# Computing the first tile of a gated elementwise kernel in four pieces of half a row in place of two rows

## Chip, cores, metric

One NeuronCore of one Trainium2 chip. The metric is the device time of one execution in microseconds (us). "Span" is the time from the first to the last instruction in a profile; the measured time is about 1.8 to 2.7 us more. The kernel before takes 935.15 us (median).

## The reference

```python
# x: 8192 x 8192, float32
def reference(x):
    a, b = np.split(x, 2, axis=-1)
    return a * (1 / (1 + np.exp(-b)))
```

268 MB are read and 134 MB are written; for each output there is one sigmoid and one multiply.

## The kernel before

The rows are cut into 32 tiles of 256 rows, two rows to a partition. A tile is one load of 8.39 MB (64 KB per partition, issued by SyncE), a sigmoid on ScalarE (ACT), a multiply on VectorE (DVE), and one store of 4.19 MB (32 KB per partition, issued by GpSimd, POOL). There are two input slots and two output slots, so loads 0 and 1 are issued at once, and load 2 waits for the last multiply of tile 0.

```python
    for i in range(n_tiles):
        ...                      # slots, views of rows and of the packed output
        load = nc.sync.dma_start(out=xs[i % SLOTS], in_=x_t[i])
        ...
        if i == 0:
            parts = [(slice(r, r + 1), slice(0, half)) for r in range(R)]      # two rows
        elif i < n_tiles - 1:
            parts = [(slice(0, R), slice(0, half))]                            # one piece
        else:
            w = half // 2                                                      # four pieces
            parts = [(slice(r, r + 1), slice(c * w, (c + 1) * w)) for r in range(R) for c in range(2)]
        for k, (r, c) in enumerate(parts):
            b = rows[:, r, 1, c]
            sig = nc.scalar.activation(out=b, in_=b, func=SIG)
            mul = nc.vector.tensor_mul(out=packed[:, r, c], in0=rows[:, r, 0, c], in1=b)
            ...                  # waits that follow from others are dropped
            if i == n_tiles - 1:
                ...              # the last tile stores each piece as it is done
        if i < n_tiles - 1:
            now["stores"].append(nc.gpsimd.dma_start(out=out_t[i], in_=os[i % SLOTS]))
```

Each odd tile's sigmoid, and each even tile's multiply, also waits for the store that had the same output slot two tiles ago.

## Time and profile before

| | kernel before |
|---|---|
| time, median of 6 (lowest to highest) | 935.15 us (935.06 to 935.74) |
| span of the profiled execution | 933.8 us |
| that execution's own time | 936.43 us |
| DVE, ACT busy | 30%, 24% |
| DMA engines busy | 9 tenths or more in 39 of 40 slices |

### The profile page before, as it was taken

The page shows a single profiled execution, that of the slowest core. Times are in us where ns is not written, and L with a number is a line of the kernel's source. Part 1 is how long each engine was busy: PE and PEld are TensorE (multiplying, and loading weights), DVE is VectorE, ACT ScalarE, POOL GpSimd, SP SyncE. Part 2 cuts the span into 40 slices and gives each one's busy share as a digit, 9 for nine tenths or more (in the row PEclk, how much of TensorE's full clock was granted, in tenths as well). Part 3 has the DMA queues.
Part 4 walks back from the last instruction along what each step waited for, and adds up shares of the span by engine and source line. Part 5 has one row for each costly group of instructions (what it writes and reads, how often), then busy time and mean ns, then how long its engine had stood idle before and what let it go on. Part 6 is the DMA issues. An engine that isn't in the chain of part 4 may idle for free.

```text
span 933.8 us, 259 instructions
## 1 busy us (share of the span) xinstructions
DVE 278.4 (30%) x36; ACT 226.6 (24%) x37; POOL 17.9 (2%) x37
## 2 busy tenths in 40 slices
DVE  0333213332133331333312333123331233311333
ACT  1223330233302333113331133311333203332023
POOL 0000000000000000000000000000000000000000
DMA  9999999999999999999999999999999999999998
GB/s 404 415 437 428 446 428 431 432 439 448 414 459 410 441 434 428 446 422 453 410 455 417 430 445 430 446 417 459 410 446 425 431 444 446 430 414 459 408 448 362
DMA packets 9649, 402.67 MB, mean 431 GB/s; under 512 B 1072, under 2 KB 1072, under 8 KB 1072
## 3 DMA queue, kind: packets, MB, share of 16 engines
q1 hardware_dynamic: 4896, 270.53, 67.1%
q0 software_dynamic: 4752, 132.12, 32.8%
q14 instruction: 1, 0.01, 0.0%
HBM read 268.44 MB, written 134.22 MB: 431 GB/s over the span
## 4 chain that ended last, share of the span: by engine, by line
DMA 73%; DVE 15%; ACT 12%; DVEq 0%; issue 0%; ACTq 0%
DMA x_sb<-in_x_dram 73%; DVE o_sb L68 15%; ACT x_sb L67 12%; DVEq L145 0%; ACTq L67 0%
## 5 line engine op out<-in xcount | busy, mean ns | idle before, releaser
L68 DVE TENSOR_TENSOR o_sb<-x_sb 128x8192 f32<-128x8192 f32 (+2 forms) x36 | 278.4, 7743 | 648.4 <-ACT x_sb L67 648.4
L67 ACT ACTIVATE x_sb<-x_sb 128x8192 f32<-128x8192 f32 (+2 forms) x36 | 225.3, 6269 | 696.0 <-DMA x_sb<-in_x_dram 696.0
L84 POOL DMA_DIRECT2D out_dram<-o_sb x31 | 16.7, 537 | 886.5 <-DVE o_sb L68 886.5
L67 ACT ACT_TABLE_LOAD x1 | 1.3, 1283 | 0.8 <-PEq L162 0.8
L81 POOL DMA_DIRECT2D out_dram<-o_sb x2 | 1.1, 533 | 18.6 <-DVE o_sb L68 18.6
L162 POOL MEMSET const-float32-0.0<- 128x1 f32 x1 | 0.1, 99 | 0.2 <-issue 0.2
L162 POOL MEMSET const-bfloat16-1.0<- 128x1 bf16 x1 | 0.1, 102 | 0.0
L162 POOL MEMSET const-float32-1.0<- 128x1 f32 x1 | 0.1, 99 | 0.0
L162 POOL MEMSET const-uint8-127<- 128x1 uint8 x1 | 0.1, 99 | 0.0
## 6 DMA issues: line engine op xcount, KB each, us to landing
out_dram<-o_sb POOLq DMA_DIRECT2D x31, 4096.0 KB, 36.1
out_dram<-o_sb POOLq DMA_DIRECT2D x2, 1024.0 KB, 5.3
out_dram<-o_sb SPq DMA_DIRECT2D x2, 1024.0 KB, 6.2
x_sb<-in_x_dram SPq DMA_DIRECT2D x32, 42.2
```

The costliest lines, as they stand in the source:

```text
L67: sig = nc.scalar.activation(out=b, in_=b, func=SIG)
L68: mul = nc.vector.tensor_mul(out=packed[:, r, c], in0=rows[:, r, 0, c], in1=b)
L81: store = queue.dma_start(out=out_t[i, :, cols], in_=os[i % SLOTS][:, cols])
L84: now["stores"].append(nc.gpsimd.dma_start(out=out_t[i], in_=os[i % SLOTS]))
L162: nc = _bacc.Bacc("TRN2", target_bir_lowering=False, num_devices=1)
```

## The change

The first tile takes the branch of the last tile: four sigmoids and four multiplies of half a row each in place of two and two of a row. A shorter first piece lets DVE start sooner, so tile 0 is finished sooner, and load 2 and store 0, which wait for it, are issued sooner.

```diff
-        if i == 0:
-            parts = [(slice(r, r + 1), slice(0, half)) for r in range(R)]
-        elif i < n_tiles - 1:
+        if 0 < i < n_tiles - 1:
             parts = [(slice(0, R), slice(0, half))]
         else:
             w = half // 2
```

## The prediction

> **What bounds the kernel now.** I read the page first, for the busy shares and the chain, then the chain in order of time, then the timeline of the start and of the end, and last the DMA of chosen stretches.
>
> The page says that no compute engine is near its limit, and that the DMA engines are full in all but the last of the 40 slices:
>
> ```profile
> DVE 278.4 (30%) x36; ACT 226.6 (24%) x37; POOL 17.9 (2%) x37
> ...
> DMA  9999999999999999999999999999999999999998
> ...
> DMA 73%; DVE 15%; ACT 12%; DVEq 0%; issue 0%; ACTq 0%
> ```
>
> The last line is a trap. The chain gives 27% of the span to DVE and ACT, which looks as if faster computing would shorten the end. The chain in order of time shows why it would not:
>
> ```profile
> 0.79 45.20 DMA x_sb<-in_x_dram
> ...
> 46.01 7.04 ACT x_sb L67
> ...
> 53.07 8.70 DVE o_sb L68
> ...
> 61.79 42.20 DMA x_sb<-in_x_dram
> ```
>
> The load issued at 61.79 takes 42.20 us to land, but the other slot's load is ahead of it in the same queue: that one lands at 75.0 (its sigmoid starts at 75.02), so this load only has the stretch from 75.0 to 104.0 for itself. A tile that is computed sooner would let its load wait longer in the queue, and it would land at the same time. The test is the DMA engines' share, stretch by stretch (columns: stretch, its length, busy time and count of DVE, ACT and POOL, clock, DMA share, GB/s):
>
> ```profile
> 0.00:34.60 34.60, 8.76 (x2) 8.40 (x3) 0.20 (x4) 1.00 1.00 424
> 34.60:46.00 11.40, 0.00 (x0) 0.00 (x0) 0.67 (x1) 1.00 0.96 365
> 46.00:62.00 16.00, 8.69 (x1) 7.03 (x1) 0.00 (x0) 1.00 1.00 432
> 62.00:75.00 13.00, 0.00 (x0) 0.00 (x0) 0.53 (x1) 1.00 1.01 436
> 75.00:104.00 29.00, 8.69 (x1) 7.03 (x1) 0.53 (x1) 1.00 1.00 434
> ```
>
> The share is 1.00 from the start, while tile 0 is being computed, because loads 0 and 1 are both in the queue. A pair of tiles takes 58.0 us (62 to 120 in the chain), so a tile takes 29.0 us, and its 8.39 MB in and 4.19 MB out at 434 GB/s take 12.58/0.434 = 29.0 us. The kernel is bound by the transfers: all of 402.67 MB at 434 GB/s is 927.8 us of the 933.8 us span. The 6 us left are the first issue (0.8), a loss of about 2 us where the first store joins the loads (11.4 us at 365 in place of 434 GB/s is 0.79 MB, or 1.8 us), and the tail.
>
> [...] from 75 to 104 us the load queue moved 8.39 MB in 64 KB packets and the store queue 4.19 MB in 32 KB packets, exactly two to one. [...]
>
> **The change part by part.** It touches tile 0 alone. Two sigmoids and two multiplies of 128x4096 become four and four of 128x2048. The load of tile 0 (one 8 MB transfer) and its store (one 4 MB transfer, after the last multiply) stay as they are; the order of instructions on all other tiles, and what they wait for, is unchanged in the compiled kernel. Added: 2 ACT and 2 DVE instructions, no DMA.
>
> The last tile already runs in these four pieces, so the cost is in the trace, above what the start has now (start, length, engine, line):
>
> ```profile
> 21.90 7.12 ACT L67 ACTIVATE x_sb<-x_sb 128x4096 f32<-128x4096 f32 x2 [19.83 <-DMA x_sb<-in_x_dram]
> 25.55 8.76 DVE L68 TENSOR_TENSOR o_sb<-x_sb 128x4096 f32<-128x4096 f32 x2 [25.55 <-ACT x_sb L67]
> 34.62 0.67 POOL L84 DMA_DIRECT2D out_dram<-o_sb  x1 [34.17 <-DVE o_sb L68]
> ...
> 916.02 7.31 ACT L67 ACTIVATE x_sb<-x_sb 128x2048 f32<-128x2048 f32 x4 [21.97 <-DMA x_sb<-in_x_dram]
> 917.96 8.90 DVE L68 TENSOR_TENSOR o_sb<-x_sb 128x2048 f32<-128x2048 f32 x4 [15.19 <-ACT x_sb L67]
> ```
>
> Now: 25.55 + 8.76 - 21.90 = 12.41 us from the first sigmoid to the end of the last multiply. In four pieces: 917.96 + 8.90 - 916.02 = 10.84 us. ACT has 0.19 us more to do and DVE 0.14 us, but DVE starts 3.65 - 1.94 = 1.71 us earlier. Tile 0 is done 1.57 us earlier, at 32.74 in place of 34.31, and with it load 2 and store 0 are issued 1.57 us earlier, the store at about 33.05.
>
> What of this lies on the path that sets the end? Load 2 gains nothing: load 1 is in the queue ahead of it until about 46 us, so load 2 waits 13 us instead of 12. Store 0 starts to share the DMA engines earlier, but these are at share 1.00 with loads in that stretch. Each byte that the store moves early is a byte that load 1 moves later. The bytes are the same, the engines are busy all the time, and so the sum to first order is 0.0 us of the 1.57.
>
> Second order: load 1 lands later by at most what the store takes from it. At one third for the store that is 1.57/3 = 0.5 us, or one store packet (4.19 MB / 128 = 32 KB; 16 engines at 434 GB/s make 27.1 each, so 1.2 us), or nothing[...]. With a period of 29.0 us all later landings move by the same amount, and the last tile's computing, which follows the last landing, moves with them. In return the stores are ahead by as much, so less of store 30 is left over in the tail, where the DMA share is still 0.92 to 0.99 from 916 to 930. These two cancel except for the last piece's latency: I put the net at between 0 and +0.6. Against it, the loss of 1.8 us where the first store comes in [...] could shrink or grow by up to a packet. That I can't place.
>
> **The rivals.** (1) The 1.57 us come through whole: 933.6. That needs the DMA engines to wait for tile 0. For it speaks the chain, where ACT and DVE stand in every round; against it the share of 1.00 up to 34.6. (2) The earlier store takes a packet from load 1, the tail doesn't give it back, and all landings move: +1.2, so 936.4. For it speaks that the end follows the last landing by a fixed chain (916.0, four pieces, last store); against it the tail's own backlog of stores. (3) The first store's entry is cheaper or dearer at its new place: -1.2 to +1.2, so 934.0 to 936.4. For it speaks the dip to 365 GB/s, which shows that something is lost there; nothing tells how it depends on the moment. (4) A new wait, as a slot freed later or a store queue that runs dry: load and store issues depend on the last multiply alone, as before, and a steady store is issued 7.1 us before the one ahead of it lands (36.1 less 29.0), so there is slack of some us against a shift of 1.57 + 1.2. I give it little.
>
> **Range and chances.** The repeats lie within 0.2 us[...]. I take 935.2, that is no change, with 933.6 (rival 1 whole, or rival 3 at its best) to 936.7 (rivals 2 or 3 at their worst, and a little spread). 2% is 18.7 us, more than the whole computing of tile 0 (12.4 us), so even the most favourable case can't be faster by 2%, and nothing seen costs that much: faster 0.003, same 0.994, slower 0.003.
>
> **What would show it right or wrong.** In the profile after: four sigmoids from 21.9 and four multiplies ending near 32.7; store 0 issued near 33.05 with a landing time a little over its 34.5 us; load 2 with a longer time to landing than its 40.7 us; sigmoid of tile 1 starting at 46.0 to 47.2 and then a period of 58.0 us per pair, at 434 GB/s; a dip below 434 just after the first store again, moved earlier. A last landing at 916.0 to 917.2 and a span of 932 to 935 confirm that the gain is absorbed. I'd be wrong if the landings from tile 1 on came 1.5 us earlier (then the queue did wait for tile 0), or if the period itself changed.

The forecast's sum came to 0.0 us of the 1.57 to first order and to 0 to +0.6 us with the second, and was put down as no change, 935.2, within 933.6 to 936.7. The width of that range is the author's estimate. What the profiles do show: from 75 to 104 us in the kernel before each of the two queues moved 144 packets, with 66.7% and 33.5% of the engines' time; in the list of single packets a 64 KB packet took 2.42 us and a 32 KB packet 1.21. A sigmoid of 2048 columns took 1897 ns and one of 4096 took 3608, so two halves took 2 x 1897 - 3608 = 186 ns more than the whole. How the loss at the first store's entry depends on its moment is not shown.

## The result

| | before | changed |
|---|---|---|
| time, median of 6 (lowest to highest) | 935.15 us (935.06 to 935.74) | 934.64 us (934.09 to 935.67) |
| ratio | | 0.9994, 95% interval 0.9982 to 1.0007 |
| span of the profiled execution | 933.8 us | 932.4 us |
| last multiply of tile 0 ends | 34.31 us | 32.80 us |
| store 0 issued | 34.62 us | 33.11 us |
| load 1 landed, sigmoid of tile 1 starts | 46.01 us | 44.85 us |
| load 31 landed, first sigmoid of the last tile | 916.02 us | 914.82 us |

The ratio is the mean time of one kernel's fast runs over that of the other's of the same rounds, so not quite the ratio of the two medians. The time is the same within the noise.

The timeline of the start in the changed kernel (start us, us, engine, line, operation; in brackets the engine's idle time before it and what ended it) shows that the compute did what was expected:

```profile
21.95 7.31 ACT L65 ACTIVATE x_sb<-x_sb 128x2048 f32<-128x2048 f32 x4 [19.89 <-DMA x_sb<-in_x_dram]
23.90 8.90 DVE L66 TENSOR_TENSOR o_sb<-x_sb 128x2048 f32<-128x2048 f32 x4 [23.90 <-ACT x_sb L65]
33.11 0.67 POOL L82 DMA_DIRECT2D out_dram<-o_sb  x1 [32.67 <-DVE o_sb L66]
44.85 7.03 ACT L65 ACTIVATE x_sb<-x_sb 128x8192 f32<-128x8192 f32 x1 [15.58 <-DMA x_sb<-in_x_dram]
```

From the first sigmoid to the last multiply it is 23.90 + 8.90 - 21.95 = 10.85 us, against 12.41 before: 1.56 us saved. The DMA of the stretches in the changed kernel, with the same columns as in the prediction, shows that the DMA engines were busy with load 1 in that time:

```profile
0.00:34.60 34.60, 8.90 (x4) 8.60 (x5) 0.87 (x5) 1.00 1.00 424
34.60:46.00 11.40, 0.00 (x0) 1.15 (x1) 0.00 (x0) 1.00 1.04 414
46.00:104.00 58.00, 17.38 (x2) 13.96 (x3) 1.07 (x2) 1.00 1.00 434
```

One thing is not as predicted. The profiled spans differ by 1.4 us, load 1 landed 1.16 us earlier rather than later, and all later landings came earlier with it. This looks deceptively like the whole saving passed on to the end. A start 1.5 us earlier was the prediction's own sign of being wrong. The experiments had to decide between two readings:

- **CHAIN**: the end follows tile 0's end one to one, as the chain of the page suggests; the saving was passed on.
- **PACKET**: the DMA engines are full anyway; the end moves only by how the first store falls in between the load packets, and this was to explain the 1.4 us.

### The profile page after: what moved, and what is told of

It is laid out like the page before. It is cut to its first block, busy times and chain, and to the rows that moved or that the text cites. A ratio compares the mean times of both kernels' runs of the same rounds, so it can differ in the third digit from the quotient of the medians.

```text
span 932.4 us, 263 instructions
## 1 busy us (share of the span) xinstructions
DVE 278.6 (30%) x38; ACT 226.8 (24%) x39; POOL 17.9 (2%) x37
## 2 busy tenths in 40 slices
DMA packets 9649, 402.67 MB, mean 432 GB/s; under 512 B 1072, under 2 KB 1072, under 8 KB 1072
## 4 chain that ended last, share of the span: by engine, by line
DMA 73%; DVE 15%; ACT 12%; DVEq 0%; issue 0%; ACTq 0%
DMA x_sb<-in_x_dram 73%; DVE o_sb L66 15%; ACT x_sb L65 12%; DVEq L143 0%; ACTq L65 0%
## 5 line engine op out<-in xcount | busy, mean ns | idle before, releaser
L66 DVE TENSOR_TENSOR o_sb<-x_sb 128x8192 f32<-128x8192 f32 (+1 forms) x38 | 278.6, 7344 | 647.1 <-ACT x_sb L65 647.1
L65 ACT ACTIVATE x_sb<-x_sb 128x8192 f32<-128x8192 f32 (+1 forms) x38 | 225.6, 5951 | 694.5 <-DMA x_sb<-in_x_dram 694.5
## 6 DMA issues: line engine op xcount, KB each, us to landing
out_dram<-o_sb POOLq DMA_DIRECT2D x31, 4096.0 KB, 34.5
```

## The experiments

All times are medians; each ratio is to the kernel before, run in the same rounds. "Landed" is the start of the sigmoid that waited for that load in the profile. Results were right unless it says otherwise.

| run | store 0 issued | load 1 landed | load 31 landed | span of the profile | time, median | ratio, 95% interval |
|---|---|---|---|---|---|---|
| no compute on tile 0 | 22.77 | 49.86 | 914.15 | 933.0 | 935.20 | 1.0004 (0.9991 to 1.0017) |
| eight pieces | 32.47 | 44.92 | 915.70 | 933.3 | 935.17 | 0.9995 (0.9981 to 1.0008) |
| changed, again | 32.99 | 44.98 | 915.77 | 933.4 | 934.78 | 0.9996 (0.9984 to 1.0009) |
| before, again | 34.68 | 45.88 | 915.89 | 933.5 | 936.10 | 1.0004 (0.9991 to 1.0018) |
| changed, store late | 34.72 | 43.75 | 913.70 | 932.6 | 934.65 | 0.9993 (0.9980 to 1.0006) |
| one piece | 37.80 | 41.08 | 912.71 | 932.7 | 935.20 | 0.9999 (0.9987 to 1.0012) |

Store 0 moves over 15 us in this table, and the time does not follow it.

### Tile 0 in one piece, and in eight

```diff
-        if 0 < i < n_tiles - 1:
+        if i < n_tiles - 1:                       # one piece
```

> Tile 0 in one piece: from the steady rows its sigmoid takes 7.03 us and its multiply 8.69, so it ends 15.8 us after its load's landing, at 37.7 us, and store 0 is issued near 38.0, 3.4 us later than in the kernel before and 4.9 later than in the changed one. CHAIN theory (the end follows tile 0's end one to one): span 937.2, 3.4 us over the kernel before, time near 938.5. PACKET theory (the DMA engines are full anyway; the end depends only on how the first store falls between the load packets, which are 2.4 us apart): load 1 lands between 43.5 and 46.5, earlier rather than later since the store takes less from it, span within 1.5 us of the kernel before, time 934 to 936.

935.20 us (934.91 to 935.52), against 935.22 of before in the same rounds. Tile 0 was done 3.2 us later than in the kernel before, and nothing was lost. CHAIN falls here. Of the PACKET range one number was missed: load 1 landed before the 43.5 to 46.5 that I expected. The profile shows the trade in full: load 1 landed at 41.08, 4.9 us earlier than before, for want of a store to share with; load 31 landed 3.3 us earlier, at 912.71; but from there to the end it took 932.7 - 912.7 = 20.0 us in place of 933.8 - 916.0 = 17.8, as more of the stores was left over. So an earlier last landing does not always bring an earlier end. The profiles fall in two groups. Where load 31 landed at 914.8 or later (both of the kernel before, both of the changed one, eight pieces, and the second run with load 2 late) the span ended 17.6 to 17.8 us after it, so there the end did follow the landing. Where it landed by 914.2 (one piece, store late, no compute) the end came 18.9 to 20.0 us after it, with stores left over. Two runs fit neither group: 17.9 us after 914.72 (the first run with load 2 late) and 18.9 us after 914.95 (the kernel before with the store later, below).

A still later store 0 might cost something, which no run tests: a line of this timeline shows that tile 3's sigmoid waited for a store last, and not for its load:

```profile
100.18 7.03 ACT L65 ACTIVATE x_sb<-x_sb 128x8192 f32<-128x8192 f32 x1 [22.16 <-DMA out_dram<-o_sb]
```

For eight pieces:

```diff
+        elif i == 0:
+            w = half // 4
+            parts = [(slice(r, r + 1), slice(c * w, (c + 1) * w)) for r in range(R) for c in range(4)]
```

> Tile 0 in eight pieces of a quarter row: DVE starts about 1.05 us after the landing and ends at about 32.2 us, store 0 is issued near 32.5, 0.6 us before the changed kernel and 2.1 before the kernel before. CHAIN theory: span 931.7, time near 933. PACKET theory: anything from 932 to 934 for the span, with load 1 landing at either 44.8 to 45 (all DMA engines change over in step, as in the changed kernel) or 46 and more (some change over a packet earlier than others).

935.17 us (934.05 to 935.37). Tile 0 took 22.98 + 9.17 - 21.89 = 10.26 us, 0.6 less than in four pieces, and the end did not move. PACKET's numbers hold; CHAIN's 933 was not reached in any of five runs.

### Only the store late, only load 2 late

To tell which of the two earlier issues could matter, each was put back alone, by a filler on DVE after the last multiply that the one has to wait for and the other hasn't.

```diff
+        if i == 0:                                # store late; load late has xs[0]
+            late = os[0][:, :2900]
+            nc.vector.tensor_copy(out=late, in_=late)
```

> The changed kernel with one more DVE copy, of part of the output tile onto itself, between the last multiply of tile 0 and store 0[...]: store 0 is issued near 34.7 as in the kernel before, load 2 stays at 32.8 as in the changed one. If the store's moment makes the difference (PACKET): load 1 lands near 46.0 with one straggling DMA engine, span 933.5 to 934. If load 2's moment makes it: span stays near 932.4. The result stays right.

934.65 us, the most even of all kernels (934.49 to 934.73), with the store issued at the old moment, 34.72, after a copy of 1.66 us. The PACKET expectation was wrong in both its numbers: I expected a landing near 46.0 and a span of 933.5 to 934, and load 1 landed at 43.75 with a span of 932.6. By what I had written down, this span spoke for the moment of load 2, which the next two runs test. The first profile's 46.01 does not belong to the moment of the store as such (see the straggler below).

> The counterpart: the DVE copy is of part of the input tile onto itself, so load 2 waits for it (issued near 34.4 as in the kernel before) and store 0 does not (issued at 33.1 as in the changed one). PACKET: as the changed kernel, load 1 landing near 44.8, span 932 to 933. If load 2's moment makes the difference: span near 933.8. The result stays right, the copied part is dead data.

935.72 us (934.93 to 936.40). The profile, of the fastest run, has load 1 at 44.70 and a span of 932.6, as PACKET had it; the median is a microsecond above that of the changed kernel, but within the spread of the kernel before (up to 935.78 in these rounds, 936.57 in others). As a test of load 2 alone this run was spoilt by my filler. Its timeline shows that GpSimd's issue of the store, which ran beside the copy, took 1.39 us in place of 0.67:

```profile
32.63 1.67 DVE L83 COPY x_sb<-x_sb 128x2900 f32<-128x2900 f32 x1
33.02 1.39 POOL L85 DMA_DIRECT2D out_dram<-o_sb  x1 [32.58 <-DVE o_sb L66]
34.32 0.33 SPq L52 DMA_DIRECT2D x_sb<-in_x_dram  x1
```

The issue ends at 34.41, just after the copy's end at 34.30. Why the issue took longer beside the copy is not shown. So I took a multiply as filler, which is another kind of instruction, on dead input data; at the 2.29 us that a multiply of 2048 columns took here, 1450 columns were estimated at 1.6 us:

```diff
+        if i == 0:
+            dead = xs[0][:, :1450]
+            nc.vector.tensor_mul(out=dead, in0=dead, in1=dead)
```

> The earlier run with load 2 late was spoilt: the DVE copy overlapped GpSimd's issue of store 0, which took 1.39 us in place of 0.67. Here the filler is a multiply ([...]on dead input data) of about 1.6 us, so store 0 is issued as in the changed kernel (33.0, taking 0.67) and load 2 only near 34.4. PACKET theory: as the changed kernel, 934.1 to 935.8, load 1 landing at 44.8 to 45.0. If load 2's moment matters: half a us or more above the changed kernel, over 935.3 in the median.

The filler took 1.66 us (32.77 to 34.43), and the issue of the store beside it (from 33.16) 0.67 again. 934.97 us (934.48 to 935.64), ratio 0.9994, the same ratio as the changed kernel's; load 1 landed at 45.06, and the median is under the 935.3 at which I had said the moment of load 2 would matter. No effect of it can be seen: it stands in the queue behind load 1 for more than 10 us either way.

### Tile 0 not computed at all

```diff
+    nc.vector.memset(os[0], 0.0)
...
+        if i == 0:
+            parts = [(slice(0, 1), slice(0, 8))]
```

> The extreme: tile 0 isn't computed but for one multiply of 8 columns, its output buffer is zeroed beforehand (wrong result for tile 0, on purpose). Store 0 and load 2 can be issued near 22.5, 10.5 us before the changed kernel. CHAIN theory: about 10 us faster, 924. PACKET theory: nothing, or slower: load 1 now shares the DMA engines from the start and lands near 48 to 49, the store queue has nothing left before tile 1 is done, and the time is 934 to 937.

The result is wrong for tile 0, on purpose. 935.20 us against 935.18 of before: taking away the whole computing of tile 0, all but one small sigmoid and multiply, gains nothing, though store 0 and load 2 were issued at 22.77 and 22.49. (One of its six runs was 938.5, one of before in the same rounds 937.14.) Load 1 landed at 49.86, a little after the 48 to 49 that I expected and 3.9 us later than in the kernel before, with store 0 in its queue from 22.77 on; store 1 was issued only at 65.92, and load 2 landed 23.1 us after load 1 in place of 29. The sum came out the same:

```profile
22.77 0.67 POOL L86 DMA_DIRECT2D out_dram<-o_sb  x1 [22.34 <-DVE o_sb L70]
49.86 7.03 ACT L69 ACTIVATE x_sb<-x_sb 128x8192 f32<-128x8192 f32 x1 [27.59 <-DMA x_sb<-in_x_dram]
914.15 7.31 ACT L69 ACTIVATE x_sb<-x_sb 128x2048 f32<-128x2048 f32 x4 [21.64 <-DMA x_sb<-in_x_dram]
```

This is the clearest evidence for the first-order step of the prediction.

### A control in which the DMA engines do wait

If the saving is hidden only because load 1 keeps the engines busy, it must come out when load 1 is held back. One added wait does that:

```diff
         now["loads"].append(load)
+        if i == 1:
+            m = gone[0]["muls"][-1]
+            tc.add_manual_dep(load.ins, m.ins.name, DEP, reason="...")
```

> A control in which the DMA engines do wait for tile 0: the kernel before (two pieces), with load 1 made to wait for the last multiply of tile 0, so the queue is empty from load 0's landing (about 21.9 us) until tile 0 is done (34.3). Idle DMA time is about 12.4 us plus the 1.8 us that a load needs from issue to landing beyond its bytes, so the time should rise by 12 to 17 us to 947 to 952. Both theories say so; this is the base for the next run.

> The same control with tile 0 in four pieces, as the change has it. If the change saves 1.57 us of tile 0 and this is hidden in the real kernel only because the DMA engines have load 1 to work on (PACKET theory), it must show here: 1.6 us less than the two-piece control, give or take a packet's 1.2 us. If the change is worth nothing for another reason (the pieces not really sooner, or the first store the one that counts), it is 0 here too.

The 1.8 us in the first expectation are those of load 0 in the kernel before: issued at 0.79, landed at 21.90, which is 21.1 us, against 8.39/0.434 = 19.3 for its bytes.

| | two pieces | four pieces |
|---|---|---|
| time, median of 4 | 950.56 us | 949.64 us |
| lowest to highest | 950.35 to 963.85 | 948.68 to 950.35 |
| load 1 issued | 34.28 us | 32.70 us |
| load 31 landed | 929.26 us | 927.83 us |
| span of the profile | 948.1 us | 946.7 us |

The DMA share of the two-piece control between 20 and 36 us:

```profile
20.00:36.00 16.00, 8.76 (x2) 7.12 (x2) 0.67 (x1) 1.00 0.18 61
```

The share is 0.18 where the real kernel has 1.00, and the time rises by 15 us. In this setting the four pieces gain 1.4 us in the profiles and 0.9 us in the medians (one run of 963.85 of the two-piece control is an outlier that the median ignores). The profile agrees with the expected 1.6; four runs that spread over 1.7 us don't fix the size better than "about one to one and a half". So the same change is worth about a microsecond where the engines wait, and nothing that can be seen where they don't.

### The noise, and the straggler

> The changed kernel again, for the noise. The first profile of the kernel before came from an execution of 936.43 us, 1.2 above its median, while that of the changed kernel was typical, so most of the 1.4 us between the two profiles should be that execution's bad luck: median 934.2 to 935.4, and its spans spread over more than 1 us. A real gain of 0.5 us would show as a ratio near 0.9994 again, luck as anything from 0.999 to 1.001.

934.78 us (934.12 to 935.79), ratio 0.9996. Its profile fell on a run of 935.79 us, with a span of 933.4, as long as the kernel before. So the 1.4 us between the first two profiles were mostly luck: over all executions whose span was recorded, the median span is 932.6 us for the kernel before (34 of them) and 932.4 for the changed one (11). So PACKET is not needed for the 1.4 us; what stays of it is that the engines are full (share 1.00) and that the store's packets come in as load packets end: in the changed kernel the sixteen load packets that started at 35.39 to 36.10 us ended at 38.80 to 39.54, and the store's first sixteen started at 38.80 to 39.54.

> The kernel before, run as if it were an experiment: true ratio 1. What its ratio and interval show is the floor under which no difference in this study means anything; I expect within 0.0007 of 1. In its profile load 1 may land at another time than the 46.0 of the first profile, if the straggling DMA engine was chance: 43 to 46, with a span of 932.4 to 933.2 as in its timed runs.

The ratio of the kernel before to itself was 1.0004, and its median here was 936.10, so medians of five move by a microsecond with the luck of the draw. (The span of its profile, 933.5, lay above the 932.4 to 933.2 that I expected; the straggler was there again.) Over all rounds, 11 of 40 executions of the kernel before and 3 of 11 of the changed one were above 935.6, the same share.

What was different at the start? On the two queues the trace lists 1072 packets of 4 bytes for 67 loads and stores, 16 for each, and those of a load run just before the sigmoid that waits for it (load 0: 20.93 to 21.53 us, sigmoid at 21.90). I read them as one from each of the 16 DMA engines, at the end of its share. The records for load 1 in the kernel before, first from 42.4 to 43.6 us and then from 43.6 to 47:

```profile
DMA packets 30, 0.49 MB, mean 410 GB/s; under 512 B 15, under 2 KB 15, under 8 KB 15
DMA packets 33, 1.57 MB, mean 463 GB/s; under 512 B 1, under 2 KB 1, under 8 KB 1
```

Fifteen engines were done by 43.6; the sixteenth reported between 45.6 and 45.8, and the sigmoid of tile 1 waited for it until 46.01. In the changed kernel, from 43.6 to 44.4:

```profile
DMA packets 32, 0.52 MB, mean 655 GB/s; under 512 B 16, under 2 KB 16, under 8 KB 16
```

All sixteen came together. So fifteen engines did land later in the changed kernel, by about 1 us, as the prediction had it for all; but the landing is set by the last one. "Before, again" shows the same straggler, between 45.4 and 45.6. The start times of the store's packets show what it did: in the kernel before the first packet of store 0 ran at 39.04 on one engine and from 41.37 to 42.25 on the other fifteen; in the changed kernel it ran from 38.80 to 39.54 on all sixteen. One engine let the store in one load packet (2.4 us) sooner than the others did.

> The kernel before with store 0 issued about 0.7 us later (a DVE copy of 1000 columns onto itself between the last multiply and the store), load 2 unchanged. The kernel before shows executions near 935.1 and others near 936.2, and in both profiles of slow ones a single DMA engine let the store in one load packet sooner than the other fifteen and landed 2.1 to 2.2 us after them. If that is a matter of the store becoming ready just at the packet boundary, 0.7 us later it is clear of it: all engines in step, load 1 landing near 43.6, no execution above 935.7, span near 932.6, as in the run with the store late on the changed kernel. If the straggler is chance of another kind: again some executions near 936.

```diff
+        if i == 0:                                # on the kernel before
+            late = os[0][:, :1000]
+            nc.vector.tensor_copy(out=late, in_=late)
```

The first half came true: with the store issued at 35.19 in place of 34.62 no engine straggled, and load 1 landed at 43.86. The second half did not: 935.70 us, with three of five runs at 935.70, 935.74 and 935.96. Its profile is of the slowest, span 933.8, and there the time was lost elsewhere: from load 1 to load 31 it took 914.95 - 43.86 = 871.09 us, where the kernel before took 916.02 - 46.01 = 870.01. So the straggler at the start is real, but it is not what makes slow executions slow in general. In "changed, again", a slow one too, load 1 landed only 0.1 us later than in the first profile of the changed kernel, but load 31 0.95 us later: these landings, too, slipped in the course of the run. Why they slip is open.

### Storing the pieces one by one

```diff
-            if i == n_tiles - 1:
+            if i in (0, n_tiles - 1):
...
-                queue = nc.sync if k >= len(parts) - 2 else nc.gpsimd
+                queue = nc.sync if i and k >= len(parts) - 2 else nc.gpsimd
...
-        if i < n_tiles - 1:
+        if 0 < i < n_tiles - 1:
             now["stores"].append(...)
```

> The next step in the change's direction: tile 0 in four pieces, each stored as soon as it is multiplied (four stores of 1 MB in 8 KB packets from about 26.4 us on, in place of one at 33.1). If the first store's moment set the end, up to 6.6 us faster. PACKET theory: 934 to 937, the loads lose to the stores what the stores gain; with 8 KB packets against 64 KB the store gets a smaller share while both queues are busy.

955.43 us (954.98 to 955.96), ratio 1.0212 (1.0199 to 1.0225): 20 us slower. My range was far off, though the expectation named the reason in its last clause. The DMA queues of this kernel from 40 to 60 us (queue: packets, MB, share of the 16 engines' time):

```profile
q1 hardware_dynamic: 128, 7.34, 84.7%
q0 software_dynamic: 128, 0.92, 10.9%
```

In these 20 us the two queues moved the same number of packets, 128 each. With 64 KB packets of loads against 8 KB of the stores the store queue got a ninth of the bytes, not a third. In the kernel before, with 64 KB against 32 KB, it was 144 packets each from 75 to 104 us, and 66.7% and 33.5% of the engines' time. So while the queues moved packets one for one, the packets' sizes decided the shares. The last piece, issued at 32.97, took 57.3 us to land. Tile 2's multiply had to wait for it, since it needs the output slot, and from then on the kernel never recovered. The waits of the whole run (engine, line, what for: us in total, times, longest):

```profile
ACT x_sb L65 <- DMA out_dram<-o_sb: 372.0, 14, 27.9
ACT x_sb L65 <- DMA x_sb<-in_x_dram: 340.2, 18, 23.5
DVE o_sb L66 <- DMA out_dram<-o_sb: 31.4, 1, 31.4
```

In the kernel before, ACT waited for loads alone. Here half of its waiting is for stores: the store queue is behind by as much as the two output slots allow, in every round. From load 1 (43.19) to load 31 (932.43) a tile takes (932.43 - 43.19) / 30 = 29.64 us in place of 29.00, which makes 30 x 0.64 = 19 of the 20 us. The engines' share is still 1.00, but from 104 to 900 us they move 425 GB/s in place of 434. The queue lines of the two pages, this kernel and then the kernel before, show where the 2% went:

```profile
q1 hardware_dynamic: 4896, 270.53, 67.4%
q0 software_dynamic: 5184, 132.12, 32.1%
q1 hardware_dynamic: 4896, 270.53, 67.1%
q0 software_dynamic: 4752, 132.12, 32.8%
```

For the same bytes the packets of the loads took 0.674 x 953.8 = 643 us in place of 0.671 x 933.8 = 627 us, 16 us more, and those of the stores 306 us in both. In the list of single packets that the trace keeps, every 64 KB packet of a load in the kernel before takes 2.42 us once the first store has come in (from 46 us on); here, after 70 us, 703 of them take 2.5 to 3.4 us. So the time is lost in stretched load packets, like those at a first store's entry (see "The dip" below). Why the packets stretch is not shown.

## Why the prediction was right

- **The bound.** It said that the DMA engines are full from the start and that the 1.57 us saved would be absorbed. Measured: 1.56 us saved on tile 0, and 0.5 us between medians with a ratio whose interval includes 1. Shown by experiment: no computing at all (935.20), one piece (935.20), and the control, in which about a microsecond of the saving comes out once the engines wait.
- **Load 2.** It said that load 2 gains nothing. Issued late alone, it gave the changed kernel's ratio, 0.9994.
- **Load 1.** It said that load 1 would land at 46.0 to 47.2. It landed at 44.85. The step "later by what the store takes" was right for fifteen engines and wrong for the landing, as the kernel before had one straggling engine at 46, which I took for all sixteen.
- **Store 0.** It said that store 0 would take a little over 34.5 us to land; it took 33.4. The straggler is only part of this: with the store at the old moment and no straggler (the two runs with the store later) it took 34.2 and 33.9. The larger part is the wait before its first packet, which ran 5.7 us after the issue in the changed kernel (33.11 to 38.80), and 6.8 us after it in the run with the store late (34.72 to 41.54).
- **All later landings and the end.** It said that the last landing carries the last tile with it, partly offset by fewer leftover stores. It put the last landing at 916.0 to 917.2; it came at 914.82 (915.77 in the repeat). With the stores behind by more, as in the one-piece run, two thirds of the gain are offset: 3.3 us earlier landing, 2.2 us longer tail.
- **The dip.** It read the 365 GB/s between 34.6 and 46 us as a loss of 1.8 us where the first store joins the loads. The loss is there, but its size was misread: packets come in bursts of 16 x 64 KB = 1 MB each 2.4 us, so the average of an 11 us window depends on which bursts it cuts. The single packets in the traces show the loss. When the first store comes in, one 64 KB packet of the load on each engine takes 3.3 to 3.6 us in the changed kernel and mostly 3.2 to 4.2 in the kernel before, in place of 2.42. Summed over the 16 engines and divided by 16, this is 1.0 us in the changed kernel and 1.35 in the kernel before. The run without computing has it too, 0.95 us, but where its store comes in, at 26 to 29.5 us; between 34.6 and 46 us it moves 420 GB/s.
- **The rivals.** Rival 1 (933.6, whole saving) fell with the one-piece and the no-compute run. Rival 2 (+1.2) did not occur. Rival 3, an entry that is cheaper or dearer, did occur, but is small: with the 1.0 us in place of 1.35 and the median spans of 932.4 and 932.6 it is worth some 0.2 to 0.3 us. The straggler is one engine on which the entry fell a packet sooner. Rival 4, a store queue that gets in the way, did not occur in the change, but it did in the run that stores the pieces one by one.

What of the half microsecond between the medians? The two sets of the changed kernel gave 0.9994 and 0.9996, the kernel before against itself 1.0004, and every interval includes 1. Yet 7 of the 11 executions of the changed kernel are below the lowest of the 40 of the kernel before (934.94), so the typical execution does seem to be a little shorter. But some 0.3 us of the 0.5 lie outside the span, and so before the first instruction or after the last: the measured time exceeds the span by 2.52 to 2.66 us in all 34 executions of the kernel before on record, and by 1.89 to 2.48 in the 11 of the changed one, while the median spans differ by 0.2 us. Why the time outside the span differs is open.

## What to carry to other kernels

Before you shorten compute that stands in the chain of waits, look at whether the DMA engines have anything else to do in that time: a wait for a load that itself stood in a queue was not a delay that faster compute could remove (here, at a share of 1.00, taking away the computing of tile 0 gave 935.20 us against 935.18). When two queues share the engines, do not make the packets of one much smaller than those of the other, even for one tile: here 8 KB against 64 KB left the store queue 10.9% of the engines' time, it never caught up, and the kernel took 20 us more. And when an effect of a microsecond in a thousand is at stake, look at the profiled execution's own time first, and run the unchanged kernel against itself.
